# Weight roundings, kept weights, the split of head outputs and a head's last scaling, ordered behind the latest eviction or head step

## Chip, cores, metric

The kernel runs on one core of a Trainium2 chip. The metric is the device time of one execution in microseconds (us), lower is better; a kernel's figure is the median of its runs. TensorE (PE) does the matmuls, VectorE (DVE), ScalarE (ACT) and GpSimd (POOL) the elementwise work, and SyncE (SP) issues most DMAs.

## What is computed

One layer of a decoder trunk on 1040 tokens (1024 and 16 meta tokens) of width 1024, in float32. The mixer adds an HGRN2 recurrence with four heads and a pooling branch with four groups, each through its own projection and a sigmoid gate; a gated MLP with a causal convolution follows.

```python
u = rmsnorm(h, mix_norm_pre[l])
proj = u @ w_in[l]
q, f_logit, i_in, g_out, v_pool, gate_a, gate_b = jnp.split(proj, cuts, axis=-1)
a = hgrn2(q, f_logit, i_in, g_out, lbs[l], hgrn_out_norm[l])   # chunks of 64, state per head
p = multiscale_pool(v_pool, pool_proj[l], pool_scale[l])       # windows 2, 4, 8, 16
z = (sigmoid(gate_a) * (a @ w_branch_hgrn[l]) + sigmoid(gate_b) * (p @ w_branch_pool[l]))
h = h + rmsnorm(z @ w_out[l], mix_norm_post[l])
u = rmsnorm(h, ffn_norm_pre[l])
gt = causal_dwconv(u @ ffn_w_gate[l], ffn_conv_w[l], ffn_conv_b[l])
y = (gelu(gt, approximate=True) * (u @ ffn_w_up[l])) @ ffn_w_down[l]
h = h + rmsnorm(y, ffn_norm_post[l])
```

In `hgrn2` each head's output is divided by its root mean square, `o * rsqrt(mean(o * o) + EPS)`, and multiplied by a gain and by `sigmoid(g)`.

## The kernel before

Activations lie with channels on the partitions and tokens along the free axis (1026 tokens of a projection, in three chunks of 342 that fill three PSUM banks). A float32 product is made of three matmuls on rounded operands: each operand is split into a high part, rounded to PE's 32-bit input format, and the low rest, and `hi*hi + hi*lo + lo*hi` is summed. So every weight tile costs a cast on ACT (`whi <- wraw`) and a subtraction on DVE (`wlo <- wraw, whi`); `wsplit` (L153, L154) does that for one block, `wsplit2` (L163, L164) for a pair of blocks of a branch projection in a tile of 1024 columns.

The stages are: norms, features, values and gates (up to 330 us); the stage that the list `ORDER` names (330 to 560 us); the output projection; the MLP as Strassen products; the down projection. The change lies in the `ORDER` stage. A word of `ORDER` is a job of PE, or a step of other work:

- `PV`, `G`, `PP`: projections of pooling values, output gates, and the four small pool projections (`ppp` banks). `BB0..7` and `BA0..7`: the two branch projections, eight blocks of 128 columns each (`pbb` and `pba` banks). The letters `a`, `b` (or `p` to `s`) cut a job into parts between which other words stand. After a job's last part `post(banks)` evicts the banks: for `PP` by L842 (ACT, `uhi`) and L843 (DVE, the low part, into `uhi` as well), for `BB` and `BA` by L881 (DVE, `sa` times the bank).
- `h0` to `h3`: the next step of that head (`head_steps`, a generator). Its steps grow decayed keys and queries level by level (L676 k, L682 q, L684 f) between small score matmuls (`sl`, L693/L699; L714 copies scores into `near`), transpose the keys, build chunk states (`ds`), scan them on DVE (L774, `st`), make the output (`po`, L792; L794 copies it to `o`; L795 squares it; L835/L836 split the squares into `rh` and `rl`), sum squares with matmuls against ones (`ms`, L801/L802), take Ln (L803) and Exp (L804) on ACT, and scale `o` (L805, DVE).
- `sp`, `sa`: the split of a pooled group or of a head's output into `ah` (L835, ACT) and `al` (L836, DVE).
- `w0` to `w5`: `keep` (in `keep_first` for 0 to 3, in steps of `keep_unit` for 4 and 5), which rounds weights of the later MLP, or sums of their quarters (L922) (cast L924 on ACT, rest L925 on DVE), and leaves them in `owed`; `pay()` later issues their stores to DRAM (`kept0h` and so on, L939), which free the buffers.

Only PE's order is set by hand here (`manual_schedule(engines={E.PE})`). The order on ACT, DVE and SP is decided by a scheduler's own timeline when the program is built; an instruction can be bound behind another by `tc.issue_after`. Each engine then works its list strictly in order. There are three rotating tiles each of `wraw`, `whi` and `wlo`, so loads, roundings, matmuls and stores wait for one another through them.

## Time and profile before

| what | us |
|---|---|
| runs | 1306.92, 1309.96, 1309.26 |
| median | 1309.26 |
| the profiled execution | 1309.94 |
| its span in the profile | 1308.2 |
| PE busy | 1288.7 (99% of the span) |
| DVE busy | 964.1 |
| ACT busy | 524.8 |
| POOL busy | 355.5 |

The profile shows one execution. A row of a timeline gives the start, the duration, the engine, the line of the kernel, the operation with output and inputs, and in brackets how long the engine had stood before and what ended that wait. A number behind x says how many equal instructions the row groups. PEclk is the share of full speed that PE's clock was granted.

### The profile page before, as it was taken

How to read it: one execution, taken by the hardware profiler on the slowest of the kernel's cores; microseconds unless marked ns; L12 is line 12 of the kernel's file. 1: busy time of each engine (PE TensorE's matmuls, PEld its weight loads, DVE VectorE, ACT ScalarE, POOL GpSimd, SP SyncE). 2: the span in 40 equal slices, each digit the busy share in tenths (PEclk: the TensorE clock that was granted, in tenths of full speed). 3: DMA queues.
4: the chain of work that ended last, by engine and by line, in shares of the span. 5: the costliest groups of instructions: out<-in, count | busy, mean ns of one | idle time of the engine just before them, and what ended most of it. 6: DMA issues, size and time to landing. Idle time of an engine off the chain costs nothing.

```text
span 1308.2 us, 21960 instructions
## 1 busy us (share of the span) xinstructions
PE 1288.7 (99%) x8650; PEld 1137.8 (87%) x8650; DVE 964.1 (74%) x1296; ACT 524.8 (40%) x905; POOL 355.5 (27%) x307
## 2 busy tenths in 40 slices
PE   8999999999999999999999999999999999999998
PEld 6799899999999898978898888888888888888886
DVE  6768965554776877765588999888898985455758
ACT  5554433332244646236663222322322232444443
POOL 3015433130000000150045555553755652000000
PEclk9999999999999999999999999999999999999999
DMA  8135543325514767766777777668776799666644
GB/s 277 42 106 164 189 156 108 121 89 151 170 63 151 226 241 239 282 222 242 243 256 250 200 206 193 164 180 208 168 180 157 152 265 290 208 225 226 228 171 161
DMA packets 143801, 247.62 MB, mean 189 GB/s; under 512 B 11000, under 2 KB 75164, under 8 KB 143698
## 3 DMA queue, kind: packets, MB, share of 16 engines
q1 hardware_dynamic: 127026, 213.42, 48.5%
q0 software_dynamic: 12064, 24.38, 11.4%
q10 hardware_dynamic: 4608, 8.41, 1.7%
q8 instruction: 68, 1.11, 0.3%
q14 instruction: 35, 0.29, 0.1%
HBM read 174.11 MB, written 95.09 MB: 206 GB/s over the span
## 4 chain that ended last, share of the span: by engine, by line
PE 89%; DVE 5%; ACT 2%; issue 2%; DMA 2%; POOL 0%; DVEq 0%; SPq 0%; ACTq 0%; POOLq 0%
PE P L307 16%; PE P L308 16%; PE P L310 16%; PE pd L187 5%; PE pd L188 5%; PE pd L189 4%; PE pm L187 2%; PE pm L189 2%; PE pm L188 2%; PE ppv L207 1%; PE pba L207 1%; PE pv L188 1%; PE pba L208 1%; PE ppv L211 1%; PE pg L207 1%
## 5 line engine op out<-in xcount | busy, mean ns | idle before, releaser
L308 PE MATMUL P<-v,whi 128*128 128x512 f32 (+2 forms) x408 | 140.7, 353 | 0.0
L307 PE MATMUL P<-v,whi 128*128 128x512 f32 (+2 forms) x408 | 140.7, 352 | 0.0
L310 PE MATMUL P<-v,wlo 128*128 128x512 f32 (+2 forms) x424 | 135.1, 349 | 0.0
L278 POOL TENSOR_TENSOR swa<-wraw,wraw 128x512 f32<-128x512 f32 x32 | 49.4, 1545 | 192.8 <-DMA wraw<-in_w_in_dram 76.7
L252 ACT CAST whi<-wraw 128x512 fp32r<-128x512 f32 x90 | 53.1, 618 | 101.7 <-PE P L308 86.9
L1525 DVE TENSOR_TENSOR rot<-wraw,rot 128x1024 fp32r<-128x1024 f32 x31 | 38.0, 1224 | 72.3 <-ACT rot L1524 72.2
L307 PEld LDWEIGHTS P<-v,whi 128*128 128x128 f32 x408 | 76.7, 188 | 10.4
L308 PEld LDWEIGHTS P<-v,whi 128*128 128x128 f32 x408 | 76.6, 188 | 10.2
L310 PEld LDWEIGHTS P<-v,wlo 128*128 128x128 f32 x424 | 74.0, 188 | 10.8
L189 PE MATMUL pd<-rot 128*128 128x512 f32 x274 | 82.5, 388 | 0.0
L188 PE MATMUL pd<-rot 128*128 128x512 f32 x274 | 82.5, 387 | 0.0
L187 PE MATMUL pd<-rot 128*128 128x512 f32 x274 | 81.9, 388 | 0.1
L253 DVE TENSOR_TENSOR wlo<-wraw,whi 128x512 fp32r<-128x512 f32 x86 | 75.2, 897 | 2.7 <-ACT whi L252 2.7
L253 DVE TENSOR_TENSOR wlo<-swb,whi 128x512 fp32r<-128x512 f32 x64 | 68.6, 1080 | 8.7 <-ACT whi L252 8.7
L252 ACT CAST whi<-swa 128x512 fp32r<-128x512 f32 x64 | 38.1, 619 | 91.7 <-PE P L308 77.7
L1524 ACT CAST rot<-wraw 128x1024 fp32r<-128x1024 f32 x31 | 32.7, 1054 | 90.8 <-PE pd L189 89.5
L307 PE MATMUL P<-uhi,whi 128*128 128x258 f32 (+2 forms) x240 | 68.6, 303 | 0.3 <-DVE sg L862 0.3
L308 PE MATMUL P<-ulo,whi 128*128 128x258 f32 (+2 forms) x240 | 68.4, 303 | 0.0
L252 ACT CAST whi<-swb 128x512 fp32r<-128x512 f32 x64 | 38.1, 618 | 70.1 <-PE P L308 65.1
L307 PE MATMUL P<-t2h,whi 128*128 128x258 f32 (+2 forms) x228 | 65.3, 304 | 0.4 <-DVE sg L864 0.4
L1453 DVE SCALAR_TENSOR_TENSOR y<-g,par,y 128x1024 f32<-128x1024 f32 x44 | 65.0, 1476 | 0.8
L307 PE MATMUL P<-t4h,whi 128*128 128x258 f32 (+2 forms) x228 | 65.5, 304 | 0.0
(388 smaller groups left out, 3837.4 us busy)
## 6 DMA issues: line engine op xcount, KB each, us to landing
wraw<-in_w_in_dram SPq DMA_DIRECT2D x36, 512.0 KB, 4.6
yt<-ysum SPq DMA_DIRECT2D x33, 512.0 KB, 5.6
wraw<-in_ffn_w_gate_dram SPq DMA_DIRECT2D x26, 512.0 KB, 7.4
wraw<-in_ffn_w_up_dram SPq DMA_DIRECT2D x22, 512.0 KB, 7.0
wsum<-in_ffn_w_down_dram SPq DMA_DIRECT2D x22, 512.0 KB, 8.9
wraw<-in_w_out_dram SPq DMA_DIRECT2D x18, 512.0 KB, 5.1
ysum<-ys SPq DMA_DIRECT2D x11, 768.0 KB, 6.0
sa<-sscr SPq DMA_DIRECT2D x16, 513.0 KB, 6.7
```

The lines of the kernel that those rows point to most:

```text
L187: pe.matmul(ps, ahi, bhi, start=first, stop=False)
L188: pe.matmul(ps, ahi, blo, start=False, stop=False)
L189: pe.matmul(ps, alo, bhi, start=False, stop=last)
L207: pe.matmul(ps[:, :n], whi[:, k, :], xhi, start=(k == 0), stop=False)
L252: act.copy(hi, src)
L253: (pool_e if 4 <= i < 2 * self.early else dve).tensor_tensor(lo, src, rr(hi), ALU.subtract)
L278: pool_e.tensor_tensor(s1, a21, a22, ALU.add)
L307: pe.matmul(d, whi[:, k, :], xh[:, c : c + w], start=(k == 0 and onto is None), stop=False, **go)
L308: pe.matmul(d, whi[:, k, :], xl[:, c : c + w], start=False, stop=False, **go)
L310: pe.matmul(x[:, o : o + w], wlo[:, k, :], xh[:, c : c + w], start=False, stop=(k == 3), **go)
L1453: dve.scalar_tensor_tensor(a, g[:, j : j + SEQ], cvw[:, j, m : m + 1], a, ALU.mult, ALU.add)
L1525: dve.tensor_tensor(lo, src, rr(hi), ALU.subtract)
```

## The change

While the `ORDER` stage is written, ACT and DVE are wrapped (`Traced`), so that the last instruction issued on each is known. After each `post(banks)`, and after each head step that isn't the last, `mark()` notes these two instructions. `behind()` binds what is issued inside it behind the noted ones, each on its own engine. Inside it stand now: cast and subtraction of `wsplit` and `wsplit2`, all of `keep`'s sums and roundings, the split `sa`, and a head's last scaling, which becomes a step of its own (`ORDER` has one more word for each head, and some `w5` and `sa3` change places). DMA starts aren't bound. All instructions are the same in kind and number; PE's and POOL's lists are the same, those of ACT, DVE and SP are permuted between 415 and 545 us of the run before, and some PSUM banks are dealt out differently. In the changed program every instruction of ACT and DVE bears the line of the wrapper, L81, and PE's lines are 31 higher here (L207 is L238).

```diff
...
-         "Gr3 h2 PP1 Gs3 h3 PP2 h2 PP3 h3 BBa0 h1 h2 BBb0 h3 w0 BBa1 h2 BBb1 h3 w1 BBa2 h2 BBb2 h3 w2 BBa3 h2 h3 w3 "
...
+         "Gr3 h2 PP1 h0 Gs3 h3 PP2 h2 PP3 h3 BBa0 h1 h2 BBb0 h1 h3 w0 BBa1 h2 BBb1 h3 w1 BBa2 h2 BBb2 h3 w2 BBa3 h2 "
...
+
+
+class Traced:
+
+
+    def __init__(self, engine):
+        self.engine, self.last = engine, None
+
+    def __getattr__(self, name):
+        method = getattr(self.engine, name)
+        if not callable(method) or name == "dma_start":
+            return method
+
+        def issue(*a, **k):
+            self.last = method(*a, **k)
+            return self.last
+
+        return issue
...
                  pool_proj, pool_scale, w_branch_pool, w_out, ffn_norm_pre, ffn_norm_post,
                  ffn_w_gate, ffn_w_up, ffn_conv_w, ffn_conv_b, ffn_w_down, out):
     nc = tc.nc
-    act, dve, pool_e, pe = nc.scalar, nc.vector, nc.gpsimd, nc.tensor
+    act, dve, pool_e, pe = Traced(nc.scalar), Traced(nc.vector), nc.gpsimd, nc.tensor
 
     cnt = [0]
     const = ctx.enter_context(tc.tile_pool(name="const", bufs=1))
...
         return t
 
 
+    urgent = {}
+
+    def mark():
+        urgent.update((e, e.last) for e in (act, dve))
+
+    def behind():
+        order = ExitStack()
+        for ins in urgent.values():
+            order.enter_context(tc.issue_after(ins.ins))
+        return order
+
     def wsplit(src, n_k, n_c, eng=dve):
         raw = wst.tile([P, n_k * n_c], F32, tag="wraw", name=nm("wraw"), bufs=NRAW, padded_shape=[P, 1024])
         with tc.issue_after(stage["after"].ins) if "after" in stage else nullcontext():
             stage["load"] = nc.sync.dma_start(raw.rearrange("p (k c) -> p k c", k=n_k), src)
         hi = wst.tile([P, n_k * n_c], F32R, tag="whi", name=nm("whi"), padded_shape=[P, 1024])
         lo = wst.tile([P, n_k * n_c], F32R, tag="wlo", name=nm("wlo"), padded_shape=[P, 1024])
-        act.copy(hi, raw)
-        eng.tensor_tensor(lo, raw, rr(hi), ALU.subtract)
+        with behind():
+            act.copy(hi, raw)
+            eng.tensor_tensor(lo, raw, rr(hi), ALU.subtract)
         return [(hi.rearrange("p (k c) -> p k c", k=n_k), lo.rearrange("p (k c) -> p k c", k=n_k))]
 
     def wsplit2(*srcs):
...
         views = [[t[:, i * 512 : (i + 1) * 512].rearrange("p (k c) -> p k c", k=4) for t in (raw, hi, lo)] for i in range(2)]
         for (r, _, _), src in zip(views, srcs):
             stage["load"] = nc.sync.dma_start(r, src)
-        act.copy(hi, raw)
-        dve.tensor_tensor(lo, raw, rr(hi), ALU.subtract)
+        with behind():
+            act.copy(hi, raw)
+            dve.tensor_tensor(lo, raw, rr(hi), ALU.subtract)
         return [(h, l) for _, h, l in views]
 
     class Loader:
...
             pe.matmul(ps[:, :n], onesr, rl[:, lo : lo + n], start=False, stop=True)
             act.activation(rs[:, lo : lo + n], ps[:, :n], AF.Ln, bias=eps_t)
         act.activation(rs, rs, AF.Exp, scale=-0.5)
-        dve.tensor_tensor(o, o, rs, ALU.mult)
+        yield
+        with behind():
+            dve.tensor_tensor(o, o, rs, ALU.mult)
         heads[h] = dict(o=o)
 
 
...
         tiles_ = [wst.tile([P, 1024], F32R, tag="whi", name=nm("whi"))]
         tiles_.append(wst.tile([P, 1024], F32R, tag="wlo", name=nm("wlo")) if lo is None else lo)
         at = [KEPT.index(key) for key, _ in what]
-        for i, (_, src) in enumerate(what):
-            hi, lo = (t[:, i * 512 : (i + 1) * 512].rearrange("p (k c) -> p k c", k=4) for t in tiles_)
-            if isinstance(src, tuple):
-                for a, op, b in src:
-                    dve.tensor_tensor(rr(lo), rr(lo) if a is None else a, rr(lo) if b is None else b, op)
-                src = rr(lo)
-            act.copy(hi, src)
-            dve.tensor_tensor(lo, src, rr(hi), ALU.subtract)
+        with behind():
+            for i, (_, src) in enumerate(what):
+                hi, lo = (t[:, i * 512 : (i + 1) * 512].rearrange("p (k c) -> p k c", k=4) for t in tiles_)
+                if isinstance(src, tuple):
+                    for a, op, b in src:
+                        dve.tensor_tensor(rr(lo), rr(lo) if a is None else a, rr(lo) if b is None else b, op)
+                    src = rr(lo)
+                act.copy(hi, src)
+                dve.tensor_tensor(lo, src, rr(hi), ALU.subtract)
         for h, t in enumerate(tiles_):
             if len(at) == 2 and at[1] == at[0] + 1 and at[0] % 2 == 0:
                 owed.append((kept[at[0] // 2][h], rr(t)))
...
                 keep_first(i) if i < EARLY else next(keeps[i - EARLY])
                 continue
             if kind == "sa":
-                ahl[i] = split(heads[i]["o"], "a")
+                with behind():
+                    ahl[i] = split(heads[i]["o"], "a")
                 continue
             if kind == "h":
                 if i not in gens:
                     gens[i] = head_steps(i)
-                next(gens[i], None)
+                if next(gens[i], True) is None:
+                    mark()
                 if not loader.at and "after" in stage:
                     loader.ahead()
                 continue
...
                 loader.ahead()
                 pay()
                 after[kind, i] = post(banks)
+                mark()
                 if kind == "BA":
                     dve.tensor_tensor(sas[i], sas[i], sbs[i], ALU.add)
                     z[i] = sas[i]
...
             loader.ahead()
             pay()
             after[kind, i] = post(banks)
+            mark()
             if kind == "BA":
                 dve.tensor_tensor(sas[i], sas[i], sbs[i], ALU.add)
                 z[i] = sas[i]
 
+
+    urgent.clear()
 
     if TRUNC:
         close_pool("ps", "sm", "fm")
```

The first place is DVE at the third and fourth pool projection, `PP2` and `PP3` (`ppp_601` to `603` are the banks of `PP2`; `wlo_612` belongs to a `BB` weight pair, k, q and f to heads 2 and 3), before:

```order
L164 TENSOR_TENSOR wlo_612_4935<-wraw_610_4933,whi_611_4934 128x1024
L684 TENSOR_TENSOR f_560_4517<-f_560_4517 128x264
L676 TENSOR_TENSOR k_535_4342<-k_535_4342,f_534_4341 128x66x8
L843 SCALAR_TENSOR_TENSOR uhi_5_88<-ppp_601_4862,par_124,uhi_5_88 128x342
L682 TENSOR_TENSOR q_537_4344<-q_537_4344,f_534_4341 128x64x8
L714 COPY_PREDICATED near_553_4447<-mask8_159,sl_606_4884 128x16x8
L843 SCALAR_TENSOR_TENSOR uhi_5_88<-ppp_602_4863,par_124,uhi_5_88 128x342
L843 SCALAR_TENSOR_TENSOR uhi_5_88<-ppp_603_4864,par_124,uhi_5_88 128x342
```

And after:

```order
L81 SCALAR_TENSOR_TENSOR uhi_5_88<-ppp_601_4862,par_124,uhi_5_88 128x342
L81 TENSOR_TENSOR f_560_4517<-f_560_4517 128x264
L81 SCALAR_TENSOR_TENSOR uhi_5_88<-ppp_602_4863,par_124,uhi_5_88 128x342
L81 TENSOR_TENSOR k_535_4342<-k_535_4342,f_534_4341 128x66x8
L81 TENSOR_TENSOR q_537_4344<-q_537_4344,f_534_4341 128x64x8
L81 SCALAR_TENSOR_TENSOR uhi_5_88<-ppp_603_4864,par_124,uhi_5_88 128x342
L81 COPY_PREDICATED near_553_4447<-mask8_159,sl_606_4884 128x16x8
L81 TENSOR_TENSOR wlo_612_4935<-wraw_610_4933,whi_611_4934 128x1024
```

The weight rounding went from ahead of the three evictions to behind them, and k and q of head 2 stand between the second and the third.

The second place is DVE around `BB2` (`sa_640` is its eviction; k_561 and q_563 are the growth of head 3 ahead of its last level of scores but one, and `wraw` with `whi` the rest of kept weights), before:

```order
L925 TENSOR_TENSOR wraw_658_5406<-wraw_658_5406,whi_659_5408 128x512
L881 TENSOR_TENSOR sa_640_5263<-sa_640_5263,pbb_641_5265 128x342
L925 TENSOR_TENSOR wraw_658_5406<-wraw_658_5406,whi_659_5408 128x512
L881 TENSOR_TENSOR sa_640_5263<-sa_640_5263,pbb_642_5266 128x342
L881 TENSOR_TENSOR sa_640_5263<-sa_640_5263,pbb_643_5267 128x342
L676 TENSOR_TENSOR k_561_4518<-k_561_4518,f_560_4517 128x16x32
L682 TENSOR_TENSOR q_563_4520<-q_563_4520,f_560_4517 128x16x32
```

And after, with an earlier pair of kept weights now behind:

```order
L81 TENSOR_TENSOR sa_640_5263<-sa_640_5263,pbb_641_5265 128x342
L81 TENSOR_TENSOR sa_640_5263<-sa_640_5263,pbb_642_5266 128x342
L81 TENSOR_TENSOR sa_640_5263<-sa_640_5263,pbb_643_5267 128x342
L81 TENSOR_TENSOR k_561_4518<-k_561_4518,f_560_4517 128x16x32
L81 TENSOR_TENSOR q_563_4520<-q_563_4520,f_560_4517 128x16x32
L81 TENSOR_TENSOR f_560_4517<-f_560_4517 128x16
L81 TENSOR_TENSOR wraw_646_5346<-wraw_646_5346,whi_647_5348 128x512 x2
```

The growth of k and q no longer has the kept tile 658 ahead of it, and tile 646, which stood further ahead, comes behind it.

The third place is the end of the heads, first ACT (`rs_709`, `o_708`, `ah_748` or `ah_744`: head 3; `o_682`: head 2; `whi_726`: kept weights; `whi_738`: the weights of `BA2` and `BA3`), before:

```order
L803 ACT_TABLE_LOAD
L803 ACTIVATE rs_709_5684<-ms_732_5826,eps_t_75 128x342
L803 ACTIVATE rs_709_5684<-ms_733_5830,eps_t_75 128x342
L803 ACTIVATE rs_709_5684<-ms_734_5834,eps_t_75 128x342
L804 ACT_TABLE_LOAD
L804 ACTIVATE rs_709_5684<-rs_709_5684 128x1026
L924 CAST whi_726_5764<-wlo_727_5765 128x512
L835 CAST ah_748_5918<-o_708_5683 128x1026
L924 CAST whi_726_5764<-wlo_727_5765 128x512
L163 CAST whi_738_5863<-wraw_737_5862 128x1024
```

And after:

```order
L81 ACTIVATE rs_709_5684<-ms_732_5822,eps_t_75 128x342
L81 ACTIVATE rs_709_5684<-ms_733_5826,eps_t_75 128x342
L81 CAST whi_717_5718<-wlo_718_5719 128x512 x2
L81 ACTIVATE rs_709_5684<-ms_734_5830,eps_t_75 128x342
L81 ACT_TABLE_LOAD
L81 ACTIVATE rs_709_5684<-rs_709_5684 128x1026
L81 CAST ah_735_5835<-o_682_5557 128x1026
L81 CAST whi_726_5789<-wlo_727_5790 128x512 x2
L81 CAST whi_738_5858<-wraw_737_5857 128x1024
L81 CAST ah_744_5895<-o_708_5683 128x1026
```

The cast `ah` of head 3 went from between the two halves of the kept tile to behind it and behind the weights' cast, and kept casts stand among the Ln.

The same place on DVE, before (`al_749` belongs to `ah_748`):

```order
L805 TENSOR_TENSOR o_708_5683<-o_708_5683,rs_709_5684 128x1026
L881 TENSOR_TENSOR sa_728_5803<-sa_728_5803,pbb_731_5807 128x342
L922 TENSOR_TENSOR wlo_727_5765<-wraw_702_5641,wlo_727_5765 128x512
L925 TENSOR_TENSOR wlo_727_5765<-wlo_727_5765,whi_726_5764 128x512
L836 TENSOR_TENSOR al_749_5919<-o_708_5683,ah_748_5918 128x1026
L925 TENSOR_TENSOR wlo_727_5765<-wlo_727_5765,whi_726_5764 128x512
L164 TENSOR_TENSOR wlo_739_5864<-wraw_737_5862,whi_738_5863 128x1024
```

And after:

```order
L81 TENSOR_TENSOR o_708_5683<-o_708_5683,rs_709_5684 128x1026
L81 TENSOR_TENSOR wlo_727_5790<-wlo_727_5790,wraw_701_5639 128x512
L81 TENSOR_TENSOR wlo_727_5790<-wlo_727_5790,whi_726_5789 128x512
L81 TENSOR_TENSOR al_736_5836<-o_682_5557,ah_735_5835 128x1026
L81 TENSOR_TENSOR wlo_727_5790<-wraw_702_5641,wlo_727_5790 128x512
L81 TENSOR_TENSOR wlo_727_5790<-wlo_727_5790,whi_726_5789 128x512
L81 TENSOR_TENSOR wlo_739_5859<-wraw_737_5857,whi_738_5858 128x1024
L81 TENSOR_TENSOR al_745_5896<-o_708_5683,ah_744_5895 128x1026
```

`al` of head 3 went behind the kept tile and the rounding of the `BA` weights, and `al` of head 2 stands between.

## The prediction

> **What bounds the kernel now.** I read the page first, for the share of each engine:

> ```profile
> span 1308.2 us, 21960 instructions
> PE 1288.7 (99%) x8650; PEld 1137.8 (87%) x8650; DVE 964.1 (74%) x1296; ACT 524.8 (40%) x905; POOL 355.5 (27%) x307
> ```

> TensorE (PE) is busy for 1288.7 of 1308.2 us. Its instructions and their order are the same after the change, so the change can win only what PE stands idle, or runs at a lower clock, in the stretch where ACT, DVE and SP are reordered. That stretch is 415 to 545 us. The view of windows shows PE's busy time and granted clock there (columns: window; its length and PE's busy time; PEld, DVE, ACT, POOL; PEclk; DMA share; GB/s):

> ```profile
> 435.00:445.00 10.00, 7.31 (x146) 6.33 (x133) 8.45 (x18) 5.71 (x12) 0.00 (x0) 0.83 1.08 349
> ...
> 515.00:555.00 40.00, 40.00 (x253) 40.00 (x253) 30.55 (x46) 12.00 (x19) 6.14 (x4) 1.00 0.74 260
> ```

> PE loses 2.69 us in 435 to 445 and also runs at 0.83 of its clock there; after 515 it never stops, so there the change can only lose. PE's timeline (start, duration, what; idle before in brackets, with what ended it) holds six stalls between 420 and 555, all of PE's idle time there, and shows the low clock:

> ```profile
> 437.20 0.42 PE L207 MATMUL pbb<-uhi,whi 128*128 128x342 f32 x1 [1.75 <-DVE uhi L843]
> 438.09 0.40 PE L207 MATMUL pbb<-uhi,whi 128*128 128x342 f32 x1 [0.31 <-DVE near L714]
> 438.47 0.65 PE L207 MATMUL pbb<-uhi,whi 128*128 128x342 f32 x1
> ...
> 442.29 0.32 PE L801 MATMUL ms<-rh,onesr 128*128 128x342 f32 x1
> 442.45 0.31 PE L802 MATMUL ms<-rl,onesr 128*128 128x342 f32 x1
> 443.40 0.42 PE L801 MATMUL ms<-rh,onesr 128*128 128x342 f32 x1 [0.64 <-ACT rs L803]
> ...
> 468.94 1.15 PE L693 MATMUL sl<-q,k 128*64 128x64 f32 x16 [0.92 <-DVE q L682]
> ...
> 499.41 0.49 PE L792 MATMUL po<-q,st 128*128 128x128 f32 x2 [1.45 <-DVE st L774]
> ...
> 511.55 0.42 PE L801 MATMUL ms<-rh,onesr 128*128 128x342 f32 x1 [1.50 <-DVE sa L881]
> ...
> 522.00 0.32 PE L207 MATMUL pba<-ah,whi 128*128 128x342 f32 x1
> ```

> From 438.47 to 442.29 PE starts 14 matmuls of one shape in 3.82 us; the two at 442.29 and 442.45 start 0.16 apart, so at full clock the 14 need 2.2. The low clock costs 1.6. The ceiling of the gain is thus 1.75 + 0.31 + 0.64 + 0.92 + 1.45 + 1.50 + 1.6 = 8.2 us.

> **Stall 1, at 435 to 442 us.** PE waits for the evictions of the third pool projection (uhi on ACT, then the low part on DVE, L843). DVE's and ACT's timelines say why they are late:

> ```profile
> 430.87 1.23 DVE L164 TENSOR_TENSOR wlo<-wraw,whi 128x1024 fp32r<-128x1024 f32 x1 [0.72 <-ACT whi L163]
> ...
> 434.26 1.23 DVE L164 TENSOR_TENSOR wlo<-wraw,whi 128x1024 fp32r<-128x1024 f32 x1 [0.59 <-ACT whi L163]
> ...
> 436.56 0.58 DVE L843 SCALAR_TENSOR_TENSOR uhi<-ppp,par,uhi 128x342 fp32r<-128x342 f32 x1
> 437.05 0.69 DVE L682 TENSOR_TENSOR q<-q,f 128x512 f32<-128x512 f32 x1
> ...
> 433.17 1.06 ACT L163 CAST whi<-wraw 128x1024 fp32r<-128x1024 f32 x1
> 434.11 1.44 ACT L842 ACTIVATE uhi<-ppp,par 128x342 fp32r<-128x342 f32 x3
> ```

> A weight rounding of 1024 columns stands ahead of the evictions on both engines. The change puts it behind them. ACT then starts the three at 433.2 instead of 434.1, and DVE, free at 433.67 (434.26 minus 0.59), evicts the first at once, the second behind `f` at 434.7 (by the rows, 0.55 is what lies between the rounding's end at 435.4 and 436.56 beside 0.6 for k), and the third behind the growth of k and q (0.6 each, as they follow each other at 467.68 and 468.28 in the chain below) at 436.4 to 437.0. PE wants the banks at 435.45 (437.20 minus 1.75), and two matmuls apart from there at 435.85 and 436.2: two are there, the third is 0.9 late. So 2.06 becomes 0.9: a gain of 1.16. The final scaling of the first head (1.23) now stands between the earlier evictions and the first weight's low part; DVE waited 0.72 there for that weight's cast, and gets the scaling's 1.15 back ahead of those evictions, so I price it at nothing, and at 0.4 (1.15 minus 0.72) without that second cover.

> The low clock came with 2.06 us idle out of 2.64; the single stalls of 0.92, 1.45 and 1.50 show no dip. A stall of 0.9 is nearest to the first, so I take the 1.6 as gone. Bounds: 0 and 1.6. [...]

> **Stall 2** (0.64, for the Ln of the first `ms` bank). The three banks no longer wait, but the small matmuls behind them now want the banks of the first and the second Ln. Two Ln of 0.5 after the matmuls at 442.29 and 442.45 against six matmuls of 0.16 leave 0.55. Gain 0.1; between 0 and 0.64.

> **Stall 3, at 468 us.** The chain of waits before it runs through the rounding of kept weights:

> ```profile
> 455.03 1.14 ACT whi L924 x2
> 456.19 4.62 DMA kept1h<-whi
> ...
> 466.24 0.60 DVE wraw L925
> 466.84 0.84 DVE sa L881 x2
> 467.68 0.60 DVE k L676
> 468.28 0.61 DVE q L682
> 468.94 1.15 PE sl L693 x16
> ```

> A cast waits 4.6 us for a store to leave its buffer, DVE's L925 waits for the cast, and k and q of the last head wait behind L925. Afterwards both L925 of that pair stand behind k and q, and DVE's queue holds no wait for a store there. L925 takes 0.6 each and two of them leave the queue ahead of q, more than the 0.92. Gain 0.9 (0 if another late cast stands ahead). What is late next is ACT: the state copy `st` of head 2, which opens DVE's scan, now stands behind two casts that wait for stores and a load; walked through with the 4.6 above they end about 1.2 us ahead of the scan's turn (an estimate). I price that at 0, and at up to 2 without that slack.

> **Stall 4, at 499 us.** The scan of the last head waits between its steps behind other DVE work:

> ```profile
> 495.20 1.29 DVE L925 TENSOR_TENSOR wlo<-wraw,whi 128x512 fp32r<-128x512 f32 x2
> 496.41 0.72 DVE L774 SCALAR_TENSOR_TENSOR st<-st,f,ds 128x128 f32<-128x128 f32 x2
> 497.87 1.23 DVE L164 TENSOR_TENSOR wlo<-wraw,whi 128x1024 fp32r<-128x1024 f32 x1 [0.74 <-ACT whi L163]
> 499.01 0.34 DVE L774 SCALAR_TENSOR_TENSOR st<-st,f,ds 128x128 f32<-128x128 f32 x1
> ```

> The last step waited for a 1024-column rounding and its cast (0.74 + 1.14), two before it for L925 (1.2). By the order after, these leave the scan, and with them a third L925 (0.6) and the `al` of the first head (1.14): 4.8 us out. In come six steps of the sixth kept tile at 0.6: 3.6. The scan ends 1.2 earlier; I take 1.15 (0.3 left), between 1.45 and a loss (first rival).

> **Stall 5, at 511 us, and the new one at 522.** From the last head's output on, ACT works off a serial chain:

> ```profile
> 499.94 0.59 ACT L794 COPY o<-po 128x512 f32<-128x512 f32 x1 [2.10 <-PE po L792]
> 500.56 1.07 ACT L795 ACTIVATE rs<-o 128x1026 f32<-128x1026 f32 x1
> ...
> 503.65 1.05 ACT L835 CAST ah<-o 128x1026 fp32r<-128x1026 f32 x1
> 504.73 1.28 ACT L803 ACT_TABLE_LOAD   x1
> 506.02 1.42 ACT L803 ACTIVATE rs<-ms,eps_t 128x342 f32<-128x342 f32 x3
> 508.75 1.06 ACT L804 ACTIVATE rs<-rs 128x1026 f32<-128x1026 f32 x1
> ...
> 520.08 1.23 DVE L836 TENSOR_TENSOR al<-o,ah 128x1026 fp32r<-128x1026 f32 x1
> ```

> In the order after, the bank that PE wants at 511.55 (at 510.05 without its stall) is released by the first Ln of the last head, no longer by DVE's `sa`. ACT's chain to it: copy 0.6, square 1.1, `rh` 1.1, table 1.3, Ln 1.4, a weight cast 1.05, `ah` 1.05, table 1.3, Exp 1.1, table 1.3, Ln 0.5, in all 11.7 from 499.94: 511.6. So the stall stays, 1.6 instead of 1.5: a loss of 0.1 (a gain of 1.5 if the copy comes earlier, a loss of 1.5 if casts that wait for stores delay it).

> Call the end of that Ln E. PE then works on (522.00 minus 511.55) for 10.45 us until it wants `ah` and `al` of the last head. Afterwards these stand behind the last kept tiles and the next BA weights on both engines. ACT: two Ln 0.9, casts 1.1, table and Exp 2.4, `ah` of head 2 1.05, casts 1.1 and 1.05, `ah` 1.05: E + 8.7, in time. DVE: the scaling can end at E + 5.7, then seven steps, four of 0.65 and three of 1.15 (`al` of head 2, the 1024 rounding, `al`), with a short wait for a cast: E + 11.9 to E + 12.5. PE stalls 1.3 to 2.0; before, `al` was ready at 521.3, 0.7 ahead. I take 1.5. Bounds: 0 and 3.6, the latter if the low clock of stall 1 follows with its 1.6. The weight tiles behind these move too, by the one or two 1.15 us steps that now stand ahead; PE stood for none of them from 515 to 555, so I price that at 0, at 1 as the upper end.

> **The rest.** POOL's order is unchanged. On SP the kept stores leave later, and the loads of `sa` and of branch weights change places with them; none of the six stalls ends with a load, and DMA has a share of 0.74 behind 515 us, so I price this at 0 and put its failure into the first rival.

> **Sum.** -1.16 - 1.6 - 0.1 - 0.9 - 1.15 + 0.1 + 1.5 = -3.3 us. The profiled execution took 1309.94 (span 1308.2), 0.7 above the median of the runs, 1309.26. So 1306.6 against the former and **1305.9** against the median. A change of 0.2% (2.6 us) is about what this kernel's runs can tell from none; -3.3 is 0.25%.

> **Rivals.**
> - *The scan waits for a store (slower).* Place: the steps of the sixth kept tile between the last head's scan. They overwrite a buffer whose store can only be issued after roundings that now stand behind three evictions; DVE's rows of these, shown below, put its issue near 484.3 (481.70 + 1.35 + two roundings of 0.6) and the first want of the buffer near 491:

> ```profile
> 481.70 1.35 DVE L881 TENSOR_TENSOR sa<-sa,pbb 128x342 f32<-128x342 f32 x3 [0.85 <-PE pbb L211]
> ...
> 490.53 0.34 DVE L774 SCALAR_TENSOR_TENSOR st<-st,f,ds 128x128 f32<-128x128 f32 x1
> ```

>   The 4.6 above would be in time. If DVE stands there, the scan, `po` and PE stand too, and each us late is a us lost beyond the first 0.3. The other terms leave -2.2; slower than +2.6 needs this stall to be 4.8 above its 1.45, a store that lands 12 us (6.7 + 0.3 + 4.8) after its due issue: SP would have to hold the issue behind another. 1310 to 1313; chance 0.11.
> - *The low clock stays.* Two stalls of 0.9 and 0.55 follow each other within 7 us, and PE stays at half clock for the same 14 matmuls: 1.6 comes back, the sum is -1.7: 1307.6. Against it: no dip at the four other stalls. Chance 0.12. [...]
> - *Stalls 5 and new are larger*, 3.0 and 2.0 by their bounds: the sum is -1.4: 1307.9. For it: the chains are serial on ACT. Chance 0.25.
> - *The new one doesn't come and stall 5 goes too* (casts find their slots in ACT's waits): -3.3 - 1.5 - 1.6 = -6.4: 1302.9. Chance 0.14.

> **Chances.** The forecast (1304.8 to 1306.6) has 0.38. Faster: 0.38 + 0.14 = 0.52. Within 0.2%: 0.12 + 0.25 = 0.37. Slower: 0.11. The range 1302.5 to 1310.5 leaves out most of the first rival and what lies beyond the last.

> **What would show it.** Right: 435 to 445 at clock 1.00 with PE busy above 8.5; no wait of `sl` for `q` at 464; the wait of `po` for `st` below 0.5; a wait of `ms` for ACT's `rs` of about 1.6; a new wait of `pba` for `al` of 1.3 to 2.0; 520 to 555 otherwise full. Wrong: a granted clock below 1 in 435 to 445 or at 520; DVE waiting for a kept store ahead of `st`; waits of `pbb` or `pba` for weights.

## The result, and the profile after

| kernel | runs | median, us | lowest to highest, us |
|---|---|---|---|
| before | 19 | 1309.11 | 1306.92 to 1309.99 |
| changed | 19 | 1311.74 | 1308.94 to 1314.77 |

The changed kernel takes 1.0024 of the time before, with a 95% interval of 1.0017 to 1.0030: 2.6 us slower, where 3.3 us faster was forecast. Its profiled execution took 1311.46 us, with a span of 1309.7, which is 1.5 more than before.

PE's timeline of the changed kernel, the rows that begin with a stall between 420 and 570 us (start, duration, what; in brackets how long PE had stood and what ended it):

```profile
436.02 0.42 PE L238 MATMUL pbb<-uhi,whi 128*128 128x342 f32 x1 [0.58 <-DVE uhi L81]
492.33 0.49 PE L823 MATMUL po<-q,st 128*128 128x128 f32 x2 [0.57 <-DVE st L81]
506.38 0.42 PE L832 MATMUL ms<-rh,onesr 128*128 128x342 f32 x1 [2.55 <-ACT rs L81]
516.61 0.43 PE L239 MATMUL pba<-al,whi 128*128 128x342 f32 x1 [0.93 <-DVE al L81]
519.76 0.42 PE L238 MATMUL pba<-ah,whi 128*128 128x342 f32 x1 [1.62 <-ACT ah L81]
521.21 0.42 PE L239 MATMUL pba<-al,whi 128*128 128x342 f32 x1 [1.03 <-DVE al L81]
562.13 0.47 PE L218 MATMUL pm<-whi,zc 128*128 128x512 f32 x1 [0.70 <-DVE sa L81]
```

The four early stalls of before are down from 2.06 + 0.64 + 0.92 + 1.45 = 5.07 us to 0.58 + 0.57 = 1.15. Behind them 1.50 became 2.55 + 0.93 + 1.62 + 1.03 + 0.70 = 6.83. In all 6.57 us of stalls became 7.98: +1.4, which is the growth of the span. The view of windows shows both ends, and where the half clock went (columns as in the prediction: window; length and PE; PEld; DVE; ACT; POOL; PEclk; DMA share; GB/s):

```profile
435.00:445.00 10.00, 9.22 (x177) 8.23 (x177) 8.76 (x20) 8.11 (x15) 0.00 (x0) 1.00 0.83 265
515.00:555.00 40.00, 36.42 (x217) 35.62 (x216) 28.65 (x41) 9.14 (x16) 6.16 (x4) 0.96 0.79 273
...
518.68:522.09 3.41, 1.30 (x6) 1.07 (x7) 2.36 (x2) 1.03 (x2) 0.00 (x0) 1.00 0.97 316
522.09:525.50 3.41, 3.41 (x14) 3.41 (x13) 2.47 (x5) 0.62 (x1) 0.00 (x0) 0.50 0.95 338
```

The stretch from 435 to 445 was won as forecast (busy 9.22 of 10 for 7.31, clock 1.00 for 0.83). From 515 to 555, where PE never stood before, it now stands 3.6 us, and for 3.41 us from 522.09 it runs at 0.50 of its clock. At half clock 3.41 us of matmuls cost 1.7 us more (0.50 * 3.41).

### The profile page after: what moved, and what is told of

Its sections match the earlier page's. It is cut to its first block, busy times and chain, and to the rows that moved or that the text cites. A ratio compares the mean times of both kernels' runs of the same rounds, so it can differ in the third digit from the quotient of the medians.

```text
span 1309.7 us, 21959 instructions
## 1 busy us (share of the span) xinstructions
PE 1290.2 (99%) x8650; PEld 1138.7 (87%) x8650; DVE 964.7 (74%) x1296; ACT 524.5 (40%) x905; POOL 356.3 (27%) x307
## 3 DMA queue, kind: packets, MB, share of 16 engines
q10 hardware_dynamic: 4608, 8.41, 1.7%
q8 instruction: 68, 1.11, 0.3%
## 4 chain that ended last, share of the span: by engine, by line
PE 94%; DVE 2%; ACT 2%; DMA 1%; issue 0%; SPq 0%; DVEq 0%
PE P L338 17%; PE P L339 17%; PE P L341 17%; PE pd L218 5%; PE pd L219 5%; PE pd L220 5%; PE pm L218 2%; PE pm L219 2%; PE pm L220 2%; PE ppv L238 1%; PE ppv L242 1%; PE ppv L239 1%; PE pv L219 1%; PE pg L238 1%; PE pv L218 1%; PE pv L220 1%
## 5 line engine op out<-in xcount | busy, mean ns | idle before, releaser
L81 ACT CAST whi<-wraw 128x512 fp32r<-128x512 f32 (+2 forms) x140 | 96.9, 714 | 169.3 <-PE P L339 86.4
L81 DVE TENSOR_TENSOR p<-p,P 128x512 f32<-128x512 f32 (+2 forms) x122 | 83.3, 683 | 41.2 <-PE P L341 40.1
L81 DVE TENSOR_TENSOR wlo<-wraw,whi 128x512 fp32r<-128x512 f32 (+2 forms) x110 | 98.3, 913 | 13.4 <-ACT whi L81 8.1
L81 DVE TENSOR_TENSOR rot<-wraw,rot 128x1024 fp32r<-128x1024 f32 x31 | 38.0, 1225 | 72.2 <-ACT rot L81 72.2
L81 ACT CAST whi<-swa 128x512 fp32r<-128x512 f32 x64 | 38.2, 619 | 90.3 <-PE P L339 80.0
L81 DVE TENSOR_TENSOR wlo<-swb,whi 128x512 fp32r<-128x512 f32 x64 | 65.6, 1033 | 9.0 <-ACT whi L81 8.9
L81 ACT CAST rot<-wraw 128x1024 fp32r<-128x1024 f32 x31 | 32.7, 1054 | 90.8 <-PE pd L220 89.4
L81 ACT CAST whi<-swb 128x512 fp32r<-128x512 f32 x64 | 38.2, 619 | 70.6 <-PE P L339 61.2
L339 PE MATMUL P<-t4l,whi 128*128 128x258 f32 (+2 forms) x228 | 65.3, 304 | 0.0
```

Source lines behind the costliest of these rows:

```text
L81: self.last = method(*a, **k)
L339: pe.matmul(d, whi[:, k, :], xl[:, c : c + w], start=False, stop=False, **go)
```

## Why the late stalls grew: ACT's and DVE's rows

ACT of the changed kernel, from the last head's output to the second group of Ln (the last two rows are a table load and the first two Ln of head 3):

```profile
493.66 1.14 ACT L81 CAST whi<-wraw 128x512 fp32r<-128x512 f32 x2 [2.05 <-DVE wlo L81]
494.71 0.58 ACT L81 COPY o<-po 128x512 f32<-128x512 f32 x1
...
504.49 1.28 ACT L81 ACT_TABLE_LOAD   x1
505.79 0.98 ACT L81 ACTIVATE rs<-ms,eps_t 128x342 f32<-128x342 f32 x2
```

From the copy's start to the end of the first Ln are 505.79 + 0.55 - 494.71 = 11.63 us; the prediction's chain had 11.7. But the copy starts late. PE's last `po` starts at 493.32 and takes 0.39, so `o` could be copied at 493.7; ahead of it stand two kept casts that came 2.05 late. The row names a step of DVE that ended at 493.64. What held them is read from ACT in `e1`, an experiment below, where the same casts wait in the same place and the store `kept6h` is named, which has to leave their buffer:

```profile
494.97 1.14 ACT L81 CAST whi<-wraw 128x512 fp32r<-128x512 f32 x2 [1.68 <-DMA kept6h<-whi]
```

In both kernels the casts start 3.0 to 3.1 us after SP issues that store (at 490.57 in the changed kernel, at 491.94 in `e1`), and in `e1` the same step of DVE ends only at 495.02, behind the casts' start. So I put the wait down to the store in both. By these rows stall 5 of 2.55 is 1.6 of the serial chain and 0.96 of the late copy. Whether it would have been 1.6 without the late copy is another question, which `e3` and `e11` leave open.

The three waits behind it are one chain across two engines. DVE of the changed kernel (`o` at 513.00 is head 3's last scaling, `al` at 515.34 belongs to head 2 and that at 519.94 to head 3; the steps of 128x512 are the kept tile, 128x1024 the weights of `BA2` and `BA3`):

```profile
513.00 1.22 DVE L81 TENSOR_TENSOR o<-o,rs 128x1026 f32<-128x1026 f32 x1
...
515.34 1.22 DVE L81 TENSOR_TENSOR al<-o,ah 128x1026 fp32r<-128x1026 f32 x1
516.47 0.69 DVE L81 TENSOR_TENSOR wlo<-wraw,wlo 128x512 f32<-128x512 f32 x1
517.85 0.69 DVE L81 TENSOR_TENSOR wlo<-wlo,whi 128x512 fp32r<-128x512 f32 x1 [0.69 <-ACT whi L81]
518.79 1.23 DVE L81 TENSOR_TENSOR wlo<-wraw,whi 128x1024 fp32r<-128x1024 f32 x1 [0.25 <-DMA wraw<-in_w_branch_hgrn_dram]
519.94 1.22 DVE L81 TENSOR_TENSOR al<-o,ah 128x1026 fp32r<-128x1026 f32 x1
```

And ACT over the same time:

```profile
517.19 0.62 ACT L81 CAST whi<-wlo 128x512 fp32r<-128x512 f32 x1 [3.83 <-DVE wlo L81]
517.72 1.04 ACT L81 CAST whi<-wraw 128x1024 fp32r<-128x1024 f32 x1
518.67 1.04 ACT L81 CAST ah<-o 128x1026 fp32r<-128x1026 f32 x1
```

Head 3's `o` is ready at 514.2, and ACT is idle then. But the next instruction in its list is a cast of the kept tile, which needs a DVE sum that stands behind `al` of head 2. ACT stands 3.83 us, then does that cast and the weights' cast, and only then `ah`: ready at 519.7, 5.5 us after its input. `al` waits behind the weights' low part in the same way. This fixes the two waits: when `al` of head 2 lands, PE has eight matmuls, until 518.14; the chain sum + cast + cast + `ah`, begun at the same time, takes 0.6 + 0.6 + 1.0 + 1.0, until 519.7, and the difference is the 1.62. The next 1.03 is one `al` against one matmul. The same two numbers come back in every experiment that keeps this order.

The 0.70 at 562 is of another kind. The last eviction of `BA7` on DVE:

```profile
561.47 0.51 DVE L81 TENSOR_TENSOR sa<-sa,pba 128x342 f32<-128x342 f32 x1 [0.45 <-PE pba L220]
```

PE starts the first `pm` of the output projection only when this eviction has ended, at 561.98. Before, the last eviction of `BA7` hadn't begun when PE started `pm`:

```profile
560.65 0.39 PE L187 MATMUL pm<-whi,zc 128*128 128x512 f32 x1
...
560.85 0.52 DVE L881 TENSOR_TENSOR sa<-sa,pba 128x342 f32<-128x342 f32 x1 [0.45 <-PE pba L189]
```

I read this as the PSUM bank of `pm`: now the one that the eviction frees, before one that was free already. It is then not a binding, but the dealing of banks that a binding shifts. No run changed the dealing alone.

## The experiments

Twelve kernels ran. The table gives for each the median, its ratio to the kernel before on the same chip (1308.6 to 1309.1 us), PE's named stalls between 420 and 570 in the profiled execution, the windows at half clock there, and the span less the stalls less 1.7 us for each window.

| kernel | median | ratio, 95% | stalls, us | half-clock windows | span less both |
|---|---|---|---|---|---|
| before | 1309.11 | 1 | 6.57 | 1 | 1299.9 |
| changed | 1311.74 | 1.0024 (1.0017 to 1.0030) | 7.98 | 1 | 1300.0 |
| e1 | 1307.11 | 0.9986 (0.9977 to 0.9994) | 3.54 | 1 | 1301.2 |
| e2 | 1311.95 | 1.0021 (1.0011 to 1.0031) | 7.72 | 3 | 1298.8 |
| e3 | 1307.59 | 0.9990 (0.9981 to 0.9999) | 3.85 | 1 | 1300.3 |
| e4 | 1313.87 | 1.0036 (1.0023 to 1.0050) | 7.90 | 4 | 1300.0 |
| e5 | 1305.73 | 0.9979 (0.9969 to 0.9988) | 3.57 | 0 | 1299.7 |
| e6 | 1311.15 | 1.0016 (1.0008 to 1.0025) | 6.01 | 2 | 1300.1 |
| e7 | 1305.91 | 0.9980 (0.9971 to 0.9989) | 4.39 | 0 | 1300.4 |
| e8 | 1307.92 | 0.9997 (0.9988 to 1.0006) | 5.02 | 1 | 1299.3 |
| e9 | 1307.54 | 0.9992 (0.9983 to 1.0001) | 4.85 | 0 | 1300.3 |
| e10 | 1307.63 | 0.9991 (0.9982 to 1.0001) | 4.77 | 1 | 1299.6 |
| e11 | 1311.80 | 1.0028 (1.0017 to 1.0040) | 8.07 | 0 | 1301.5 |
| e12 | 1303.89 | 0.9964 (0.9950 to 0.9977) | 2.10 | 0 | 1299.3 |

The last column hardly moves (1298.8 to 1301.5) while spans run from 1301.4 to 1314.7. So these two things, PE's stalls in this stretch and the windows at half clock, are what the orders differ by. `e1` and `e3` have pauses of PE besides (1.11 and 0.54 us in `e1`, 0.22 in `e3`) whose end the profile puts down to no other engine (`issue`), and which the table leaves out; with them the column is 1299.5 and 1300.0.

**Where in the program: e1 and e2.** The theory was that the bindings win in front and lose at the tail. `e1` binds only up to the word `sa1` (index 101 of `ORDER`), `e2` only from there on.

```diff
-        for ins in urgent.values():
+        for ins in urgent.values() if bound[0] else ():
...
-        for kind, i in order:
+        for word, (kind, i) in enumerate(order):
+            bound[0] = 0 <= word < 101       # e2: 101 <= word < 999
```

> The changed kernel with the binding switched off from the word sa1 on (the split of head 1), so that the words after it are ordered by the scheduler alone. By the order, ah and al of head 3 then stand ahead of the rounding of the next branch weights again; ACT's list up to the last head's first Ln is that of the changed kernel. Theory A (the loss is the order of the last splits behind weight roundings, which stops PE three times by 0.93 + 1.62 + 1.03 = 3.6 us between 515 and 522 us and brings the low clock, some 1.7 us): the waits for ah and al fall to 0.5 or less in sum, the clock is 1.00 in 515 to 535, the wait of ms for rs stays at about 2.5, and the time is 4.5 to 6 below the changed kernel, 1305.5 to 1307.5, that is 0.15 to 0.3% faster than before. Theory B (late loads and stores set the end, the splits only show it): the stalls move to waits of pba for weights or of casts for DMAs, and the time stays within 1.5 of the changed kernel, 1310 to 1313.

> The other half: binding only from the word sa1 on. The order up to there is close to that of the kernel before, and the last splits stand behind weight roundings as in the changed kernel. Theory A: the stalls of before at 435, 443, 468 and 499 us return (2.06, 0.64, 0.92, 1.45 and the low clock 1.6), the wait of ms for rs is about 1.7, and the waits for ah and al of 2.5 to 3.6 with the low clock come on top: 1312.5 to 1316, 0.25 to 0.5% slower than before. Theory B: 1309 to 1312, since the kept tiles, and so the stores and loads, keep the times of before.

`e1` took 1307.11, as theory A has it: it keeps the gain in front (a stall of 0.36 at `po`, none of `sl` for `q`) and has no wait for `ah` or `al`. Its window at half clock is at 509 to 512, and it has the two pauses named above, 1.65 in all, that no theory has. Stall 5 is still there:

```profile
507.69 0.42 PE L832 MATMUL ms<-rh,onesr 128*128 128x342 f32 x1 [2.48 <-ACT rs L81]
```

`e2` took 1311.95, a little below theory A and within theory B's range; its place speaks for A, since it has the early stalls of before and the same late waits as the changed kernel:

```profile
522.69 0.42 PE L238 MATMUL pba<-ah,whi 128*128 128x342 f32 x1 [1.62 <-ACT ah L81]
524.14 0.66 PE L239 MATMUL pba<-al,whi 128*128 128x342 f32 x1 [1.02 <-DVE al L81]
```

It has no wait of `ms` for head 3, where 1.7 was expected. So the new waits come from the bindings at the tail, and stall 5 of `e1` (2.48, against 1.50 before) from those in front.

**The tail alone: e9.** Bound as in the changed kernel, but only in the words 0 to 106. The third `w5` is word 107, so its kept tile too is unbound here, unlike what the expectation says. On ACT `ah` of head 3 stands ahead of the kept tile and the `BA` weights; the front, stall 5 included, stays.

> Bound as in the changed kernel up to and with the third w5; from BBa7 on (the last scaling of head 3, the splits sa2 and sa3, the fourth w5 and the BA weights behind it) nothing is bound. On ACT the cast ah of head 3 now stands right behind ah of head 2, ahead of the kept tile and the BA weights' cast; on DVE head 3's scaling stands ahead of two evictions of BBb7, and both al ahead of the low parts of the kept tile. All in front is as in the changed kernel, so stall 5 (ms for ACT's rs) should stay at 2.5. Theory A (the three new waits of 0.93, 1.62 and 1.03 are made by the kept tile and the BA weights standing ahead of ah and al): they shrink to 0 to 0.5 in sum, and the time is that of the changed kernel less 3.1 to 3.6, 1307.5 to 1309, about that of e1. Rival B (the waits are ACT's serial chain from stall 5 on, whatever stands between): ah and al still wait 2 us or more, 1310 to 1311.5. A half-clock window or none moves either by 1.7.

1307.54, and the three waits of 3.58 are gone but for 0.20:

```profile
507.19 0.42 PE L832 MATMUL ms<-rh,onesr 128*128 128x342 f32 x1 [2.52 <-ACT rs L81]
523.21 0.74 PE L242 MATMUL pba<-ah,wlo 128*128 128x342 f32 x3 [0.20 <-DVE wlo L81]
```

Theory A held in time and in place; a chain that only hangs on stall 5 (rival B) did not. ACT's rows show it best:

```profile
512.73 1.05 ACT L81 CAST ah<-o 128x1026 fp32r<-128x1026 f32 x1 [0.36 <-DVE o L81]
...
518.86 0.62 ACT L81 CAST whi<-wlo 128x512 fp32r<-128x512 f32 x1 [3.83 <-DVE wlo L81]
```

ACT stands for the same 3.83 us at the same cast, but `ah` of head 3 is ahead of it.

**By kind: e3, e4, e11.** Each takes `behind()` away from one kind of work and leaves it elsewhere: `e3` from the splits `sa`, `e4` from `wsplit` and `wsplit2`, `e11` from `keep`.

```diff
-                with behind():
+                with ExitStack():
                     ahl[i] = split(heads[i]["o"], "a")        # e3; e4 and e11 alike in theirs
```

> The changed kernel with the splits of head outputs (sa) not bound, all else bound. By the order, ah and al of head 3 stand between the two halves of the last kept tile, as before the change; a cast of kept weights (whi_703) now stands between the square and rh of the last head instead of ahead of its copy. Theory A: no wait for ah and al above 0.5, clock 1.00 in 515 to 535, the wait of ms for rs between 1.5 and 2.6; time 1304.5 to 1307.5. Theory B: within 1.5 of the changed kernel.

`e3`: 1307.59, 0.1 above theory A's range. No wait for `ah` or `al`, and stall 5 at 2.44 although the copy now comes when `po` is done (494.21): the two kept casts that stood ahead of it now stand inside the chain. So "late copy" and "chain" are here the same 1.0 us of casts in another place.

> The changed kernel with wsplit and wsplit2 not bound. By the order only one thing changes on ACT and nearly only one on DVE: the cast and rounding of the weight pair 611/612 stand ahead of the three evictions at 433 us again, as in the kernel before. The stall of 2.06 in two pieces at 435 to 438 us should return in place of 0.58. Theory C (the low clock hangs on that stall): the clock in 435 to 445 falls to about 0.83 and the time is 2.5 to 3.5 above the changed kernel, 1314 to 1315.5. [...]

`e4`: 1313.87, the slowest. The weights' rounding stands ahead of the evictions of `PP2` again (stall 1 is 1.73 + 0.31), the 1.62 and 1.02 stay, and four windows run at half clock, one of them at 439.8 to 443.2, behind stall 1. Its time is 0.1 below theory C's range and the low clock is at theory C's place; that the windows of one trace lie on a grid is shown in the section on the hardware. So it is the weights' binding that wins stall 1; it is not what makes the late waits.

> As the changed kernel, but the sums and roundings of kept weights are not bound; the last scaling, sa and the weights' roundings still are. DVE's rounding of the first kept tile stands ahead of the evictions of PP2 again (two steps of 0.6, and growth of head 3), the kept steps stand inside the first scan and ahead of head 3's output again, and the kept tile of the third w5 is no longer tied to the tail. Theory A (stall 5's extra 0.96 comes from kept casts that were pushed behind a late low part and so met a store that still held their buffer): ACT copies head 3's output as soon as PE has it, and the wait of ms is 1.3 to 1.8 instead of 2.55; stall 1 grows from 0.6 to 1 to 1.9; the ah/al waits of 3.6 stay if BA's weights alone make them, and halve if the kept tile does. 1308 to 1311. Rival B (stall 5 hangs on the weights' and splits' binding): the wait of ms stays at 2.4 or more, 1311 to 1313.

`e11`: 1311.80, rival B by its time, by neither theory's way. The wait of `ms` for head 3 is gone altogether; its matmuls run through, in banks dealt otherwise. In its place the kept steps stand inside the scan again, as this view of PE's waits shows (us in total, times, longest):

```profile
PE po L823 <- DVE st L81: 2.4, 3, 0.9
PE pba L238 <- ACT ah L81: 1.6, 1, 1.6
PE ms L832 <- ACT rs L81: 1.3, 2, 0.6
```

How much of stall 5 hangs on the late copy is thus not settled by this run. The `ah` wait is 1.62 once more. Of the three kinds it is thus the split's binding that makes the late waits: without it (`e3`) they are gone; with either of the others taken away instead (`e4`, `e11`) the 1.62 and 1.02 or 1.03 stay. The binding of the last scaling was not taken away alone; in `e3`, where it stays, the waits are gone.

**The serial chain: e5, e6, e7, e8.** Stall 5 is a chain on ACT with three table loads of 1.28 us between head 3's output and its Ln, two of them because Exp of head 2 stands between the Ln of head 2 and of head 3 (`e5`, where it stands behind both, has one load there). `e5` is `e1` with Exp of head 2 bound behind head 3's Ln; `e6` is the same with everything bound as in the changed kernel.

```diff
-        act.activation(rs, rs, AF.Exp, scale=-0.5)
+        heads[h]["ln"] = act.last
+        if h == 2:
+            yield
+        with tc.issue_after(heads[3]["ln"].ins) if h == 2 else nullcontext():
+            act.activation(rs, rs, AF.Exp, scale=-0.5)
...
-   BBb6 h2 w5 BBa7 h3 sa2 BBb7
+   BBb6 w5 BBa7 h3 h2 h2 sa2 BBb7
```

> As e1_bind_until_sa1, and the Exp of head 2 stands behind the Ln of head 3 (ORDER has the last two steps of head 2 behind the third last of head 3). By the order two table loads are gone from ACT, and between the last head's copy and its first Ln stand copy 0.6, square 1.1, rh 1.1, one table 1.3, four Ln 1.9, a weight cast 1.05 and ah 1.05, about 8.0 us where the changed kernel has 11.6. Theory A (the wait of ms for rs is this chain on ACT): PE's 10 us of work cover it, the wait of 2.5 falls to 0.3 or less, and with it the low clock that followed it in e1; the other waits of e1 (0.4 of po, 0.7 of pm) stay. Time 1302.5 to 1304.5, 0.35 to 0.5% faster than before. Theory B (ACT's chain only hides another late bank or a late load): the wait of ms names another releaser, and the time stays within 1.5 of e1's 1307.1.

`e5`: 1305.73, faster than both kernels. The time alone would fit theory B too, but stall 5 fell, as theory A has it, from 2.48 to 0.31, and two of PE's rows show what was late next:

```profile
503.46 0.42 PE L832 MATMUL ms<-rh,onesr 128*128 128x342 f32 x1 [0.31 <-ACT rs L81]
513.97 0.43 PE L239 MATMUL pba<-al,whi 128*128 128x342 f32 x1 [1.22 <-DVE al L81]
516.31 0.42 PE L239 MATMUL pba<-al,whi 128*128 128x342 f32 x1 [0.67 <-DVE al L81]
```

The waits for `al`, 1.89 in all, were not foreseen; theory A's range was missed by 1.2.

> The same Exp behind the Ln of head 3, on the changed kernel with all of its binding. By the order ah of head 3 stands behind the last kept tile and the cast of the next branch weights, as in the changed kernel. Theory A: the wait of ms for rs goes (2.5 to 0.3), the waits of pba for ah and al stay at 2 to 4 us in sum, since PE now comes earlier to them by as much as ACT, with a low clock in most runs: 1306.5 to 1309.5. If the two sets of stalls are one (the first delays the second), all goes: 1302.5 to 1304.5.

`e6`: 1311.15, above what was expected: `ms` waits 0.31, but `ah` 2.97, and two windows in a row run at half clock. The `ah` is head 2's this time, the first that the `BA` blocks want from these two heads, as ACT's row shows:

```profile
516.56 1.05 ACT L81 CAST ah<-o 128x1026 fp32r<-128x1026 f32 x1 [3.23 <-DVE o L81]
```

In the changed kernel it was done at 511.55. Here Exp of head 2 runs behind head 3's Ln, and the bound scaling, behind steps of the kept tile, ends on DVE only at 516.53. With the tail bound, what stall 5 gives up is taken by the next wait: PE arrives earlier, and this `ah` later.

`e7` and `e8` put two and three copies of 1026 columns into that chain, to measure its price:

```diff
+        for _ in range(2 if h == 3 else 0):     # e8: 3
+            act.copy(rs, rs)
         for lo, n in CH_Q:
             ps = bank("ms")
```

> e5_ln_before_exp with two copies of rs onto itself on ACT (1.05 us each) ahead of the first Ln of head 3, nothing else moved; the output is the same. With some 1 us of slack in e5 the wait of ms for rs should be 0.8 to 1.3 us. Theory E (the clock is granted by windows of 3.41 us on a fixed grid: half speed for one whole window after one in which PE stood for more than about 1.5 us; the traces so far show half clock for 3.41 us each time, and starts that lie whole multiples of 3.41 apart): no dip at all, so the time is e5 plus the stall, 0.8 to 1.3. Theory C (a dip hangs on a stall and grows with it): a dip too, e5 plus 2 to 3.

> e5_ln_before_exp with three such copies; by the order the two casts of a kept tile (1.15) also come ahead of that Ln, so the chain is some 4.3 us longer and the wait of ms for rs 3.0 to 3.6 us. Theory E: of a stall that long more than 1.5 us lies in one window whatever the phase, so nearly every run has a dip of 3.41 us at half clock, which costs 1.7: e5 plus 4.7 to 5.5, and the step from e7 to e8 is larger than the growth of the stall by 1.7. Theory F (a stall costs its own length alone): e5 plus 3.0 to 3.6.

`e7`: 1305.91, +0.2 for two copies. `ms` waits 0.45 longer (0.76), and the stalls sum to 0.8 more than in `e5`; the runs' mean granted clock, 0.9993 for 0.9987, offsets most of it by an estimate (half a window in each run, 0.8 us). The two profiled executions, neither with a window here, differ by 1.5. `e8`: 1307.92, +2.0 for the third:

```profile
506.70 0.65 PE L834 MATMUL ms<-rh,onesr 128*128 128x342 f32 x1 [3.38 <-DVE sa L81]
```

Its stalls add up to only 0.6 more than in `e7` (5.02 against 4.39), since the `al` waits shrink from 1.69 to 0.17; the rest is put down to one window at half clock, 1.7. That `e7` has no such window and `e8` has one is what theory E said. The times are in no theory's range: `e8` is `e5` plus 2.2, where E had 4.7 to 5.5 and F 3.0 to 3.6. Both counted the copies' length and not what stands behind.

**To a faster order: e10 and e12.** `e10` is `e5` with the third kept step written, and bound, behind the split of head 3.

```diff
-   BBb6 w5 BBa7 h3 h2 h2 sa2 BBb7 h3 BAa0 sa3 BAa1 w5 BAb0
+   BBb6 BBa7 h3 h2 h2 sa2 h3 sa3 w5 BBb7 BAa0 BAa1 w5 BAb0
...
-            bound[0] = 0 <= word < 101
+            bound[0] = word < 101 or (word > 104 and kind == "w")
...
                 with behind():
                     ahl[i] = split(heads[i]["o"], "a")
+                if i == 3:
+                    mark()
```

> e5 (Exp of head 2 behind head 3's Ln, binding off from sa1 on) with the kept tile of the third w5 written behind the split of head 3 and bound behind it, so that both scalings and both ah and al stand on DVE and ACT ahead of all six of its steps. In e5 two of these steps (0.6 each) stood ahead of head 3's scaling, and PE waited 1.22 and 0.67 for the two al. Theory A (these waits come from what stands ahead on DVE): al of head 2 comes 0.9 to 1.2 earlier and al of head 3 is in time; e5's 1305.7 less 1.2 to 1.9, 1303.8 to 1304.6. Rival B (the BA weights, whose low part now stands behind the kept tile, come late, or the waits only move to the evictions): 1305.5 to 1307. No half-clock window is expected, since no stall above 1.3 is left.

1307.63: rival B, above its 1307, with a window at half clock. `al` no longer waits; the low part of the next weights, now behind six steps of the kept tile, does:

```profile
522.67 0.74 PE L242 MATMUL pba<-ah,wlo 128*128 128x342 f32 x3 [2.33 <-DVE wlo L81]
```

`e12` puts that rounding between the two: behind the split of head 3, ahead of the kept tile.

```diff
-   sa3 w5 BBb7 BAa0 BAa1 w5 BAb0 BAb1 BA2 BA3
+   sa3 BBb7 BAa0 BAa1 w5 BAb0 BAb1 BA2 w5 BA3
...
+    done = set()
+
     def mark():
-        urgent.update((e, e.last) for e in (act, dve))
+        if not done:
+            urgent.update((e, e.last) for e in (act, dve))
...
                 with behind():
                     ahl[i] = split(heads[i]["o"], "a")
                 if i == 3:
                     mark()
+                    done.add("done")
...
-            bound[0] = word < 101 or (word > 104 and kind == "w")
+            bound[0] = word < 101 or "done" in done
```

> As e10, but the rounding of the weights of BA2 and BA3 is put right behind the two al, ahead of the kept tile, which is written behind BAa1 (its last step behind BA2), so that kept tiles and weight tiles take turns in the three buffers; from head 3's split on, everything bound is bound behind that split alone. Theory A (e10's wait of 2.33 at pba and its half-clock window came from this rounding standing behind the kept tile): the wait is gone, the al waits stay away, PE's waits are e10's others, 0.86 + 0.57 + 0.31 + 0.70 = 2.4 us, no stall is long enough for a half-clock window, and the time is e5's 1305.7 less the 1.1 by which the sum is below e5's 3.6: 1303.8 to 1305.0. Rival B (the tail only passes the wait on: the weights of BA4 to BA7 come late behind the kept tile's stores): a new wait of pba for whi or wlo of 1 us or more at 533 to 545, 1305.5 to 1307.5.

1303.89, the fastest: 0.9964 of before (0.9950 to 0.9977). Theory A held, but for a wait of 0.47 for `al`. PE's stalls are down to 2.10, none of them long:

```profile
436.07 0.42 PE L241 MATMUL pbb<-uhi,whi 128*128 128x342 f32 x1 [0.63 <-DVE uhi L81]
...
503.32 0.42 PE L835 MATMUL ms<-rh,onesr 128*128 128x342 f32 x1 [0.31 <-ACT rs L81]
513.22 0.43 PE L242 MATMUL pba<-al,whi 128*128 128x342 f32 x1 [0.47 <-DVE al L81]
...
553.78 0.47 PE L221 MATMUL pm<-whi,zc 128*128 128x512 f32 x1 [0.69 <-DVE sa L81]
```

## Why the prediction was wrong, step by step

| step | predicted | measured in the profiled runs |
|---|---|---|
| stall 1 | -1.16 | 2.06 to 0.58: -1.48 |
| low clock | -1.6 | one window before, one after: 0 |
| stall 2 | -0.1 | 0.64 to 0: -0.64 |
| stall 3 | -0.9 | 0.92 to 0: -0.92 |
| stall 4 | -1.15 | 1.45 to 0.57: -0.88 |
| stall 5 | +0.1 | 1.50 to 2.55: +1.05 |
| the new one | +1.5 | 0.93 + 1.62 + 1.03: +3.58 |
| `pm` | none | +0.70 |
| sum | -3.3 | +1.4 |

Stalls 1 to 4 gave -3.9 for -3.3: the mechanism and sizes of the front were right, though `po` kept 0.57 where below 0.5 was named as the sign.

- **The new stall failed, and weighs most.** The place was right and the mechanism in part (`al` late behind the kept tile and the weights); the size was not: 3.58 for 1.5. The upper bound of 3.6 was 2.0 of stall and 1.6 of low clock; measured are 3.58 and 1.7, 5.3 in all. The failed step is "`ah` 1.05: E + 8.7, in time". E, the end of the first Ln, was 506.34, and `ah` of head 3 ended at 519.71, E + 13.4. ACT's list was added up as if ACT were free to run it; its kept casts take their input from DVE, and the second of them stood 3.83 us for a DVE sum behind `al` of head 2. The two engines' lists were each summed, but not walked together. `al` too came late, at 521.16, E + 14.8 for E + 11.9 to 12.5. `e9` and `e3` show the cause: with `ah` and `al` ahead of these instructions, 0.20 or nothing is left.
- **Stall 5 was mis-sized**, +1.05 for +0.1. The chain of 11.7 (its terms as printed add up to 11.8) was right at 11.63; its start, taken as the moment when `po` is done, was 0.96 late behind kept casts. The prediction's upper bound named just this (a loss of 1.5 "if casts that wait for stores delay it").
- **The low clock failed as a term.** It was tied to stall 1, and 1.6 taken as gone with it. It is gone there and back at 522. The other place was in the prediction too, as a bound of the new stall, but not in the sum.
- **`pm`** was not looked at, being behind the stretch; 0.70 was lost there, by the reading above to banks dealt otherwise.

Of the rivals, the one with larger stalls 5 and new (3.0 and 2.0) is the nearest, but its other terms kept the whole gain of the clock. The scan did not wait for a store.

The profiled runs differ by 1.5 us, the medians by 2.6. The rest, as far as the runs tell, is the clock: over its 19 runs the changed kernel's mean granted clock was 0.9965 (0.994 to 0.999), while that of before, in the runs beside the experiments, averaged 0.9973 to 0.9980. One window at half clock takes 0.5 * 3.41 / 1310 = 0.0013 off the mean, so the changed kernel has on average 0.6 to 1.2 windows more, or 1.0 to 2.0 us. That is an estimate from these means; a trace shows one execution only.

## What to carry to other kernels

Where work is handed back and forth between two engines, walk both lists together: an instruction with its input ready can stand behind one whose input hangs on the other engine, as `ah` of head 3 did behind a cast for which ACT stood 3.83 us, and neither list's sum of durations shows it. The rule that puts whatever is not urgent behind the latest urgent work helped in the middle of this stage and hurt at its end, where part of what is bound (the split) is itself what PE wants next. When a stall is removed, say what PE then reaches earlier, and price stalls by how they fall together: here several in 3.41 us, 2.11 us idle in sum, cost 1.7 more by the clock.
